# Gates, branches and the last down projection with tokens in the partitions, and both parts of x in one 512-column product of the up projection, in a two-layer decoder trunk

## The chip, the core and the metric

The kernel runs on one core of one Trainium2 chip. The metric is the device time of one execution in microseconds. TensorE is called PE in the views, with its weight loads as PEld; VectorE is DVE, ScalarE ACT, GpSimd POOL, SyncE SP. SP issues the DMAs.

## What is computed

Two layers over 256 tokens of width 1024, all in float32. Each layer has a mixer part and a feed-forward part (FFN):

```python
xn = rms_norm(h, norm_mix[l])
proj = xn @ w_in[l]
(q, k, v, qi, ki, wi, sc_u, sc_b, sc_c, rw_z, gate_pre) = jnp.split(proj, split_points, axis=-1)
...
y_a = dsa_attention(q, k, v, qi, ki, wi)
y_b = short_conv_mixer(sc_u, sc_b, sc_c, sc_conv[l])
y_c = rwkv7_time_mix(rw_z, ...)
branches = jnp.stack([y_a, y_b, y_c], axis=2)
up = jnp.einsum('bsgc,gcd->bsgd', branches, w_branch[l])
gates = jax.nn.sigmoid(gate_pre + b_gate[l]).reshape(bsz, seq, N_BRANCH, D_MODEL)
mixed = jnp.sum(gates * up, axis=2)
h = h + mixed @ w_out[l]
h = h + conv_glu_ffn(rms_norm(h, norm_ffn[l]), ffn_up[l], ffn_conv[l], ffn_down[l])
```

At the end stands `rms_norm(h, norm_final)`. The attention picks 64 keys a query (top-k) with an indexer of its own; the time mixing is a recurrence over the tokens, solved in four chunks of 64; the FFN is 1024 to 2 x 2816, a causal convolution over three tokens, silu(gate) * up, and 2816 back to 1024.

## The kernel before, in words

**Numbers in two parts.** Every float32 operand of a large product is split into a high part in the fp32r format and a low part, the rest. `mm3` makes one product out of three: high weights by high x, low weights by high x, high weights by low x, all into one PSUM bank. A weight block of 128 x 1024 is loaded by SP (`weights`), its high part is a copy on ScalarE or VectorE (CAST 128x1024 in the profile), its low part a subtraction on VectorE (TENSOR_TENSOR 128x1024).

**Layout.** h and everything made from it stand with channels in the partitions and the 256 tokens in the columns. So in `proj` a 128 x 128 block of weights is loaded into PE and 256 columns of x pass it: 8 blocks x 3 = 24 products of 256 columns for 128 output channels. `gate` (8 of these for each of three branches, with the bias and tanh in one ScalarE instruction), `branch` (two outputs from one weight block, 12 products each), the output projection and the FFN's up projection (`proj` or `proj_pair`, 2 a tile) have this form; `down` adds one of 22 tiles into four banks with 24 products of 256 columns. After the last `down` of layer 1 VectorE adds the banks to h, ScalarE scales by the final norm's weights, PE transposes to tokens in partitions, the sum of squares gives the factor, and four DMAs store the result.

**FFN.** Of the 22 tiles the first three (`raw`) are computed from x before its norm is known and scaled afterwards; from the fourth on x is normed first. A tile's down projection follows its up projection by `LAG` = 3 tiles. The convolution reads the bank directly: one ScalarE product, two VectorE SCALAR_TENSOR_TENSOR of 255 and 254 columns.

**Memory.** Tiles of equal size share places, so many for each size: 20 of 4 KB a partition, 5 of 8 KB (x in its two parts, the merged sum), and smaller ones (a gate half is a tile of 1 KB). All 8 PSUM banks are one set.

**Order.** `record` writes down every operation with its dependences; `Program.plan` puts them in an order by the table `STEPS`, whose rows shift priorities, places and the choice between ScalarE and VectorE for operations that either can do; `issue` writes that one order out to all engines. Each engine takes its instructions strictly in this order.

What the change touches, with the lines of the profiled program, follows. Since `issue` writes all instructions (L735), the profile's views name that line throughout, and shapes and tiles tell them apart: `tbank` is a PSUM bank, `t` any shared place.

Of the kernel before, what the change touches and what calls it, by code (L numbers as in the profile page):

```python
# [19 lines left out]
P = 128  # L20
T = 256
# [27 lines left out]
def col_tiles():  # L49
# [8 lines left out]
    gate = lambda b: [(f"g{b}", d, r(O_GATE + DM * b + 128 * d)) for d in range(8)]  # L58
# [10 lines left out]
def branch_after(name, j):  # L69

    if name in ("g0", "g1") and j % 2:
        return [(int(name[1]), j // 2)] + ([(2, dd) for dd in range(4)] if name == "g0" and j == 7 else [])
    return []
# [65 lines left out]
def unit_list():  # L139

    units = []
    for l in range(L):
        for name, j, cols in col_tiles():
            units += [KT * 128]
            units += [4 * 256] * len(branch_after(name, j))
# [8 lines left out]
for _u in UNITS:  # L154
# [4 lines left out]

STEPS = [  # L160
    (1, '', 0, 0, 0, 0, 0), (1, 'ACT', 0, 0, 1.0, 0, 10000000), (2, '', 0, 0, 0, 0, 0), (4, 'places', 0, 0, 0, 0, 0),
    (4, 'places', 0, 0, 0, 0, 0), (4, 'places', 0, 0, 0, 0, 0), (1, 'places', 0, 0, 0, 0, 0),
    (1, 'places', 0, 0, 0, 0, 0), (2, 'engines', 990915, 0, 0.03, 0, 10000000),
    (1, 'order', 896638, 4975, 0.5, 188145, 228145), (1, 'ACT', 217391, 0, 0.3, 595554, 600554),
    (1, 'part', 0, -5023, 0, 1013, 1284), (1, 'part', 0, 4104, 0, 3504, 3576),
    (1, 'order', 923868, 7215, 0.1, 55, 5055), (1, 'part', 0, 1600, 0, 3849, 3933),
    (1, 'order', 288402, 1494, 0.3, 789264, 829264), (1, 'order', 583563, 6230, 0.5, 509266, 549266),
    (1, 'part', 0, -8415, 0, 3683, 3814), (1, 'engines', 587952, 0, 0.03, 692266, 732266),
    (1, 'order', 159137, 7905, 1.0, 706934, 711934), (2, 'kind', 386904, 1641, 0, 0, 10000000),
    (1, 'engines', 488388, 0, 0.1, 615956, 630956), (1, 'engines', 587705, 0, 0.3, 655019, 755019),  # L170
    (1, 'part', 0, -734, 0, 1757, 1772), (1, 'ACT', 181973, 0, 0.3, 693955, 708955),
    (1, 'engines', 364955, 0, 0.01, 0, 10000000), (1, 'engines', 420582, 0, 0.03, 0, 10000000),
    (1, 'engines', 896209, 0, 0.03, 715418, 720418), (1, 'order', 474360, 5710, 0.3, 684381, 699381),
    (1, 'part', 0, 14260, 0, 3707, 3736), (1, 'ACT', 373534, 0, 0.01, 0, 10000000),
    (1, 'order', 542579, 25885, 0.01, 897, 40897), (1, 'engines', 438663, 0, 0.1, 86737, 91737),
    (1, 'ACT', 41472, 0, 1.0, 672478, 712478), (1, 'part', 0, 984, 0, 2447, 2853),
    (1, 'engines', 398618, 0, 0.03, 709685, 809685), (3, 'part', 0, -19735, 0, 1058, 1090),
    (1, 'order', 665662, 2167, 0.1, 144116, 244116), (3, 'engines', 72169, 0, 0.03, 0, 10000000),
    (3, 'order', 130940, 1878, 0.01, 0, 10000000), (1, 'part', 0, 2876, 0, 3891, 4075),
    (1, 'order', 942563, 3016, 0.5, 661837, 701837), (2, 'part', 0, -15687, 0, 63, 91),  # L180
    (1, 'order', 383053, 30450, 1.0, 690456, 695456), (1, 'order', 93525, 1313, 0.01, 0, 10000000),
    (1, 'engines', 831744, 0, 1.0, 108625, 148625), (1, 'part', 0, 2048, 0, 3222, 3261),
    (1, 'engines', 80806, 0, 0.3, 710617, 810617), (1, 'order', 828966, 10709, 0.01, 681522, 721522),
    (1, 'engines', 507078, 0, 0.1, 713036, 728036), (3, 'order', 651912, 3518, 0.03, 0, 10000000),
    (3, 'part', 0, -6283, 0, 564, 651), (2, 'kind', 234875, -743, 0, 0, 10000000),
    (1, 'order', 991842, 2678, 0.03, -7909, 92091), (2, 'order', 347360, 8669, 0.5, 577409, 617409),
    (2, 'part', 0, -822, 0, 3865, 3944), (1, 'engines', 721218, 0, 0.3, 151671, 251671),
    (1, 'engines', 306551, 0, 0.03, 178872, 278872), (1, 'kind', 178191, -1522, 0, -5914, 34086),
    (1, 'engines', 419199, 0, 0.3, 581815, 621815), (1, 'ACT', 794654, 0, 0.3, 634869, 734869),
    (1, 'order', 926129, 13374, 0.03, 64910, 79910), (1, 'ACT', 428750, 0, 1.0, 531114, 571114),  # L190
    (1, 'order', 42072, 10147, 0.01, 557875, 657875), (1, 'engines', 510082, 0, 0.3, 589724, 594724),
    (1, 'part', 0, -950, 0, 3766, 3812), (1, 'order', 147063, 1704, 0.01, 0, 10000000),
    (1, 'part', 0, -19719, 0, 3229, 3240), (1, 'engines', 323590, 0, 0.3, 620245, 635245),
    (1, 'engines', 594072, 0, 0.1, 125838, 140838), (1, 'part', 0, 806, 0, 1233, 1297),
    (1, 'order', 273961, 6202, 0.1, 262736, 362736), (1, 'order', 134846, 3866, 0.01, 0, 10000000),
    (1, 'engines', 95409, 0, 0.3, 979739, 1019739), (1, 'order', 668525, 7708, 0.01, 0, 10000000),
    (1, 'engines', 706667, 0, 0.3, 720429, 725429), (1, 'order', 717637, 7122, 0.03, -19448, 20552),
    (1, 'ACT', 42008, 0, 1.0, 48246, 148246), (1, 'part', 0, -664, 0, 1602, 1651), (4, 'places', 0, 0, 0, 0, 0),
    (1, 'order', 422257, 6239, 0.01, 0, 10000000), (3, 'engines', 105424, 0, 0.1, -13940, 26060),
    (5, 'places', 0, 0, 0, 0, 0), (4, 'places', 0, 0, 0, 0, 0), (2, 'order', 545213, 9838, 0.01, 0, 10000000),  # L200
    (3, 'part', 0, 724, 0, 3539, 3542), (3, 'engines', 473114, 0, 0.03, 0, 10000000),
    (1, 'order', 628496, 37064, 0.03, 644098, 684098), (1, 'part', 0, 3151, 0, 1215, 1230),
    (2, 'order', 290810, 3456, 0.01, 0, 10000000), (3, 'order', 587523, 24879, 0.5, 615132, 655132),
    (1, 'part', 0, -891, 0, 828, 968), (1, 'order', 410355, 36181, 0.3, 603707, 618707),
    (1, 'part', 0, -3528, 0, 1066, 1082), (3, 'order', 706784, 6554, 0.5, 7180, 107180),
    (1, 'ACT', 192201, 0, 1.0, 143721, 183721), (1, 'engines', 50739, 0, 0.03, 597302, 612302),
    (1, 'engines', 703874, 0, 0.03, 0, 10000000), (2, 'engines', 276219, 0, 0.1, 845144, 945144),
    (3, 'order', 765817, 2210, 0.3, 557477, 572477), (1, 'engines', 223121, 0, 0.03, 519497, 619497),
    (1, 'order', 897640, 8500, 0.5, 570780, 610780), (1, 'order', 427450, 6044, 1.0, 705750, 745750),
    (1, 'part', 0, -3754, 0, 3054, 3165), (1, 'engines', 704649, 0, 0.3, 696412, 701412),  # L210
    (1, 'part', 0, 699, 0, 3487, 3531), (1, 'order', 329467, 13522, 0.3, 542936, 582936),
    (1, 'ACT', 810161, 0, 0.3, 473272, 513272), (1, 'order', 143890, 1733, 0.03, 0, 10000000),
    (1, 'ACT', 411363, 0, 0.3, 167522, 267522), (1, 'engines', 606894, 0, 1.0, 575128, 580128),
    (1, 'ACT', 707518, 0, 1.0, 573592, 578592), (1, 'kind', 747229, 10931, 0, 0, 10000000),
    (1, 'order', 779245, 5614, 0.1, 482972, 582972), (1, 'engines', 524910, 0, 0.3, 583218, 598218),
    (1, 'order', 990499, 32354, 0.03, 565786, 665786), (1, 'order', 211927, 3710, 0.5, 178298, 193298),
    (1, 'part', 0, 5170, 0, 553, 561), (1, 'order', 823641, 3167, 0.01, 0, 10000000),
    (1, 'order', 173100, 7368, 0.3, 666551, 706551), (1, 'kind', 268635, 3923, 0, -3950, 36050),
# [1451 lines left out]
```

## Time and profile before

| | before |
|---|---|
| device time, median of 3 runs | 987.15 us (987.07 to 987.45) |
| the profiled execution's own time | 987.48 us |
| its span, first to last instruction | 985.7 us |
| granted PE clock, mean | 0.986 |
| instructions | 21374 |
| DMA, share of 16 engines | 46.8% |

How to read it: a busy time is a share of the span in which an engine had at least one instruction under way. PE's products are pipelined, so a row's mean duration (284 ns for the commonest product) is the latency of one, and the distance between two starts is shorter. "Idle before" is the time an engine rested ahead of the rows of a group, with what ended it. The chain of waits follows the last instruction back to what released it.

### The profile page before, as it was taken

The page shows a single profiled execution, that of the slowest core. Times are in us where ns is not written, and L with a number is a line of the kernel's source. Part 1 is how long each engine was busy: PE and PEld are TensorE (multiplying, and loading weights), DVE is VectorE, ACT ScalarE, POOL GpSimd, SP SyncE. Part 2 cuts the span into 40 slices and gives each one's busy share as a digit, 9 for nine tenths or more (in the row PEclk, how much of TensorE's full clock was granted, in tenths as well). Part 3 has the DMA queues.
Part 4 walks back from the last instruction along what each step waited for, and adds up shares of the span by engine and source line. Part 5 has one row for each costly group of instructions (what it writes and reads, how often), then busy time and mean ns, then how long its engine had stood idle before and what let it go on. Part 6 is the DMA issues. An engine that isn't in the chain of part 4 may idle for free. (4 is left out here: it accounts for less than half of the span.)

```text
span 985.7 us, 21374 instructions
## 1 busy us (share of the span) xinstructions
PE 950.7 (96%) x8692; PEld 925.4 (94%) x8692; DVE 841.9 (85%) x1717; ACT 492.3 (50%) x917; POOL 27.6 (3%) x44
## 2 busy tenths in 40 slices
PE   8999999899999999999998979998999999999996
PEld 7998989899999999999998968997999999999996
DVE  7999859996798986877898997799977999978784
ACT  7954536584255555444766342473843333343443
POOL 1020010000000000000001001000000000000000
PEclk9999999999999999999999989999999999999999
DMA  9443334634653656455533412364255635655541
GB/s 318 155 150 108 100 118 151 213 107 151 211 177 127 195 191 210 164 188 195 206 130 131 169 51 81 124 209 154 99 177 185 212 115 177 211 192 178 187 151 43
DMA packets 45649, 157.93 MB, mean 160 GB/s; under 512 B 5488, under 2 KB 6768, under 8 KB 45552
## 3 DMA queue, kind: packets, MB, share of 16 engines
q1 hardware_dynamic: 45552, 156.58, 46.8%
q8 instruction: 68, 1.11, 0.5%
q14 instruction: 29, 0.24, 0.1%
HBM read 154.99 MB, written 1.05 MB: 158 GB/s over the span
## 5 line engine op out<-in xcount | busy, mean ns | idle before, releaser
L735 PE MATMUL tbank<-t,t 128*128 128x256 f32 (+5 forms) x8440 | 927.0, 276 | 19.5 <-DVE t L735 12.5
L735 PEld LDWEIGHTS tbank<-t,t 128*128 128x128 f32 (+4 forms) x8440 | 901.4, 182 | 39.5 <-issue 14.5
L735 DVE TENSOR_TENSOR t<-t,t 128x1024 fp32r<-128x1024 f32 (+12 forms) x570 | 466.1, 838 | 43.2 <-ACT t L735 34.5
L735 ACT CAST t<-t 128x1024 fp32r<-128x1024 f32 (+3 forms) x335 | 273.8, 837 | 175.7 <-DVE t L735 91.4
L735 DVE SCALAR_TENSOR_TENSOR t<-tbank,tconsts_vec,t 128x255 f32<-128x255 f32 (+1 forms) x168 | 79.4, 480 | 33.7 <-ACT t L735 31.9
L735 ACT ACTIVATE t<-t 128x256 f32<-128x256 f32 (+4 forms) x106 | 44.1, 428 | 73.1 <-DVE t L735 70.5
L735 ACT COPY t<-tbank 128x256 f32<-128x256 f32 (+3 forms) x105 | 45.7, 443 | 59.3 <-PE tbank L735 47.3
L735 DVE SCALAR_TENSOR_TENSOR t<-t,tconsts_vec,t 128x256 f32<-128x256 f32 (+3 forms) x132 | 60.0, 482 | 3.7 <-ACT t L735 3.5
L735 ACT ACTIVATE t<-tbank,tsmall_hv 128x256 f32<-128x256 f32 x64 | 29.4, 473 | 63.4 <-PE tbank L735 63.4
L735 DVE CAST t<-t 128x1024 fp32r<-128x1024 f32 (+2 forms) x86 | 50.6, 595 | 6.4 <-DMA t<-in_w_dram 4.6
L735 ACT ACTIVATE t<-tbank,tconsts_vec 128x256 f32<-128x256 f32 x59 | 27.9, 473 | 49.4 <-PE tbank L735 47.2
L735 ACT ACTIVATE t<-t,tconsts_vec 128x256 fp32r<-128x256 f32 (+1 forms) x56 | 27.0, 502 | 22.5 <-DVE t L735 22.5
L735 PE MATMUL tbank<-tconsts_cst,t 128*128 128x128 f32 (+2 forms) x168 | 27.2, 276 | 6.7 <-DVE t L735 5.3
L735 DVE TENSOR_TENSOR t<-tbank,t 128x256 f32<-128x256 f32 (+2 forms) x52 | 24.4, 478 | 8.4 <-PE tbank L735 5.3
L735 PEld LDWEIGHTS tbank<-tconsts_cst,t 128*128 128x128 f32 (+1 forms) x168 | 20.2, 153 | 8.8 <-issue 3.7
L735 DVE SCALAR_TENSOR_TENSOR t<-t,tbank 128x256 f32<-128x256 f32 x48 | 19.4, 413 | 10.5 <-PE tbank L735 10.4
L735 DVE TENSOR_TENSOR t<-t,tbank 128x256 f32<-128x256 f32 (+1 forms) x48 | 22.8, 484 | 5.9 <-PE tbank L735 5.8
L735 DVE TENSOR_TENSOR t<-t 128x256 f32<-128x256 f32 (+1 forms) x54 | 23.6, 437 | 1.6
L735 POOL TENSOR_SCALAR t<-t 64x4 f32<-64x4 f32 x16 | 10.9, 686 | 446.2 <-DVE t L735 445.4
L735 ACT ACTIVATE t<-t,tatt_mx 128x256 f32<-128x256 f32 (+1 forms) x51 | 21.6, 450 | 0.5 <-DVE tatt_mx L735 0.4
L735 DVE SCALAR_TENSOR_TENSOR t<-t,t 64x252 f32<-64x252 f32 (+3 forms) x42 | 20.4, 506 | 0.3
L735 DVE TENSOR_TENSOR t<-tbank,tconsts_cst 64x256 f32<-64x256 f32 (+1 forms) x48 | 19.3, 419 | 0.7
(85 smaller groups left out, 237.5 us busy)
## 6 DMA issues: line engine op xcount, KB each, us to landing
t<-in_w_dram SPq DMA_DIRECT2D x288, 512.0 KB, 3.6
t<-in_x_dram SPq DMA_DIRECT2D x4, 256.0 KB, 4.0
t<-in_w_dram SPq DMA_DIRECT2D x8, 128.0 KB, 3.6
t<-in_lora_dram SPq DMA_DIRECT2D x4, 256.0 KB, 6.8
out_dram<-t SPq DMA_DIRECT2D x4, 256.0 KB, 2.8
t<-t SPq DMA_DIRECT2D x4, 128.0 KB, 2.4
tconsts_cst<-in_cst_dram SPq DMA_DIRECT2D x1, 339.0 KB, 4.9
t<-in_heads_dram SPq DMA_DIRECT2D x1, 256.0 KB, 7.5
```

The costliest lines, as they stand in the source:

```text
L735: getattr(real[op.engine], name)(*map(arg, args), **{k: arg(v) for k, v in kw.items()})
```

## The change

- **By tokens.** `by_token` loads 128 tokens of x into PE as the fixed operand and lets 512 columns of weights pass: high x by high weights, high x by low weights, low x by high weights. One output is 128 tokens x 512 channels, a full bank. The gates (2 halves a branch, 2 token tiles), the branches and the last layer's down projection (`down_by_token`) take this form. The gates' bias now is a row that a DMA spreads over all partitions; VectorE adds it, ScalarE takes tanh of 1024 columns.
- The gated sum so has tokens in the partitions; PE transposes it back, 16 blocks of 128 x 128 a layer, before the output projection. That projection begins its first three outputs with the first half of the sum.
- **Both parts of x at once.** In the FFN from the fourth tile on, `wide` lets high and low x pass the high weights in one product of 512 columns, into two halves of a bank, and high x pass the low weights in one of 256 columns. The halves are added: a copy (ScalarE or VectorE) and an addition on VectorE; the convolution then reads SBUF.
- **The end.** In layer 1, 16 fp32 products by the identity put h into the down projection's banks; each token tile's banks are squared with a running sum on ScalarE, and VectorE multiplies them by the factor and the norm's row, two DMAs each.
- **Places.** The tiles of 8 KB are gone or halved; nearly all are of 4 KB and share one set. h alone keeps 8 KB.
- **Order.** `STEPS`, `plan` and the cost functions are gone; `FOUND` holds a finished order, the places and the ScalarE or VectorE choice as packed text, and `recall` reads it. `ADDED` is empty, so its branch in `weights` is never taken.

The order on PE at one tile of the second FFN, before: the last rows of a down projection (`tbank_5`, `tbank_1`) and the first of an up product (x is `t2048_4` high and `t2048_1` low, the weights `t1024_18` high and `t1024_1` low):

```order
L735 MATMUL tbank_5_10692<-t1024_4_11705,t1024_6_11845 128x256 x2
L735 MATMUL tbank_5_10692<-t1024_4_11705,t1024_16_11859 128x256
L735 MATMUL tbank_1_10699<-t1024_4_11705,t1024_6_11845 128x256 x2
L735 MATMUL tbank_1_10699<-t1024_4_11705,t1024_16_11859 128x256
L735 MATMUL tbank_4_11999<-t2048_4_10481,t1024_18_11782 128x256
L735 MATMUL tbank_4_11999<-t2048_1_10536,t1024_18_11782 128x256
L735 MATMUL tbank_4_11999<-t2048_4_10481,t1024_1_11797 128x256
```

The same place now: the last rows of an up product into `tbank_2` (`t1024_22` holds both parts of x), then the down projection by tokens:

```order
L487 MATMUL tbank_2_10579<-t1024_22_9351,t1024_7_10469 128x512
L487 MATMUL tbank_2_10579<-t1024_22_9351,t1024_25_10481 128x256
L487 MATMUL tbank_7_9524<-t1024_18_10548,t1024_2_10438 128x512
L487 MATMUL tbank_7_9524<-t1024_27_10559,t1024_2_10438 128x512
L487 MATMUL tbank_7_9524<-t1024_18_10548,t1024_2_10438 128x512
L487 MATMUL tbank_6_9531<-t1024_18_10548,t1024_2_10438 128x512
```

Three products of 256 columns became one of 512 and one of 256 in the up projection, and six became three of 512 in the down projection.

The order on VectorE in layer 1's mixers at the solve of the recurrence (`t1024_19` is its matrix, the STREAM_TRANSPOSE its last transposition), before:

```order
L735 TENSOR_TENSOR t1024_12_7724<-t1024_13_7485,t1024_7_7517 128x1024
L735 TENSOR_TENSOR t256_4_7567<-tbank_1_7679,t256_4_7567 128x256
L735 SCALAR_TENSOR_TENSOR t256_14_7765<-t256_4_7567,tconsts_vec_0_104,t256_14_7765 128x255
L735 SCALAR_TENSOR_TENSOR t256_14_7765<-t256_4_7567,tconsts_vec_0_104,t256_14_7765 128x254
L735 TENSOR_TENSOR t1024_19_7708<-t1024_19_7708,tbank_3_7767 128x16x16
L735 TENSOR_TENSOR t1024_19_7708<-t1024_19_7708,tbank_6_7787 128x16x16
L735 STREAM_TRANSPOSE t1024_9_7817<-t1024_19_7708 128x512
L735 COPY t1024_13_7862<-tbank_0_7826 32x512
```

The same place now (`t1024_26` is the matrix; MAX and MATCH_REPLACE on `tatt_isc0` and `t256_1` are the attention's top-k):

```order
L487 MATCH_REPLACE t256_1_7610<-tatt_m81_0_7809,t256_1_7610 128x256
L487 TENSOR_TENSOR t1024_26_7794<-t1024_26_7794,tbank_1_7873 128x16x16
L487 MAX tatt_m80_0_7915<-tatt_isc0_0_7745 128x8
L487 MAX tatt_m81_0_7809<-t256_1_7610 128x8
L487 TENSOR_TENSOR t1024_26_7794<-t1024_26_7794,tbank_3_7894 128x16x16
L487 MATCH_REPLACE tatt_isc0_0_7745<-tatt_m80_0_7915,tatt_isc0_0_7745 128x128
L487 STREAM_TRANSPOSE t1024_4_7924<-t1024_26_7794 128x512
L487 MAX tatt_m80_0_7915<-tatt_isc0_0_7745 128x8
```

The top-k, which came after the recurrence, now alternates with its solve.

The diff, cut to its core:

```diff
-    gate = lambda b: [(f"g{b}", d, r(O_GATE + DM * b + 128 * d)) for d in range(8)]
+    gate = lambda b: [(f"g{b}", q, list(range(O_GATE + DM * b + 512 * q, O_GATE + DM * b + 512 * q + 512))) for q in range(2)]
...
-STEPS = [
-    (1, '', 0, 0, 0, 0, 0), (1, 'ACT', 0, 0, 1.0, 0, 10000000), (2, '', 0, 0, 0, 0, 0), (4, 'places', 0, 0, 0, 0, 0),
...
+FOUND = (
...
+class Moving:
+    def __init__(self, hi, lo, tiles=()):
+        self.hi, self.lo, self.tiles = hi, lo, tiles
+    def both(self, k):
+        return self.tiles[k // 2][:, k % 2].rearrange("p a t -> p (a t)")
...
-    x8 = pool("x8", 4)
+    x8 = pool("x8", 8)
...
-    gtp = pool("gt", 10)
-    mgp = pool("mg", 1)
+    gtp = pool("gt", 3)
+    rowp = pool("row", 1)
+    mgp = pool("mg", 2)
...
+    def xpair():
+        ts = [x8.tile([P, 2, 2, T], F32R, name="x8") for _ in range(KT // 2)]
+        return Moving(lambda k: ts[k // 2][:, k % 2, 0], lambda k: ts[k // 2][:, k % 2, 1], ts)
...
+    def by_token(x, n):
+        os_ = [pm.tile([P, 512], F32, name="pm") for _ in range(2)]
+        for k in range(n):
+            if k % 2 == 0:
+                wh, wl = weights()
+            s = slice(512 * (k % 2), 512 * (k % 2) + 512)
+            for o, ts in zip(os_, (slice(0, 128), slice(128, 256))):
+                with prog.group("stream"):
+                    PE.matmul(o, x.hi(k)[:, ts], wh[:, s], start=k == 0, stop=False)
+                    PE.matmul(o, x.hi(k)[:, ts], wl[:, s], start=False, stop=False)
+                    PE.matmul(o, x.lo(k)[:, ts], wh[:, s], start=False, stop=k == n - 1)
+        return os_
+    def wide(x):
+        wh, wl = weights()
+        o = pm.tile([P, 2, T], F32, name="pm")
+        for k in range(KT):
+            s = slice(128 * k, 128 * k + 128)
+            with prog.group("stream"):
+                PE.matmul(o.rearrange("p a t -> p (a t)"), wh[:, s], x.both(k), start=k == 0, stop=k == KT - 1, skip_group_check=True)
+                PE.matmul(o[:, 0], wl[:, s], x.hi(k), start=False, stop=k == KT - 1, skip_group_check=True)
+        return o
...
-        def gate(b, d):
-            g = gtp.tile([P, T], F32, name="gt")
-            o = proj(xh, xl)
-            A.activation(g, o, AF.Tanh, bias=hv[:, 8 + 8 * b + d:9 + 8 * b + d], scale=0.5)
+        def gate(b, q):
+            bias = row("bg", 512, (l * 3 + b) * DM + 512 * q)
+            g = gtp.tile([P, 2, 512], F32, name="gt")
+            for tt, o in enumerate(by_token(xn, KT)):
+                V.tensor_tensor(g[:, tt], o, bias, OP.add)
+            A.activation(g, g, AF.Tanh, scale=0.5)
             return g
...
+        def branch(b, q, g):
+            for tt, o in enumerate(by_token(Moving(*(lambda k, t=t: t[:, k] for t in br[b])), 4)):
+                m = mg[tt][:, 512 * q:512 * q + 512]
+                if b == 1:
+                    V.scalar_tensor_tensor(m, g[:, tt], 1.0, o, op0=OP.add, op1=OP.mult)
                 else:
+                    V.scalar_tensor_tensor(g[:, tt], g[:, tt], 1.0, o, op0=OP.add, op1=OP.mult)
+                    V.tensor_tensor(m, m, g[:, tt], OP.add)
+            if b == 2:
+                for d in range(4 * q, 4 * q + 4, 2):
+                    p = pm.tile([P, 2, T], F32, name="pm")
+                    for i in range(2):
+                        for tt in range(2):
+                            PE.transpose(p[:, i, 128 * tt:128 * tt + 128], mg[tt][:, 128 * (d + i):128 * (d + i) + 128], ident)
+                    t = merged.tiles[d // 2]
+                    A.activation(t[:, :, 0], p, AF.Copy, scale=0.5)
+                    V.scalar_tensor_tensor(t[:, :, 1], p, 0.5, t[:, :, 0].bitcast(F32), op0=OP.mult, op1=OP.subtract)
...
+        def down_by_token(item, wd, tts=range(2)):
+            f, ah, al = item
+            wh, wl = wd
+            for tt in tts:
+                ts = slice(128 * tt, 128 * tt + 128)
+                for c in range(2):
+                    o, s = dn[2 * tt + c], slice(512 * c, 512 * c + 512)
+                    with prog.group("stream"):
+                        PE.matmul(o, ah[:, ts], wh[:, s], start=f == 0, stop=False)
+                        PE.matmul(o, ah[:, ts], wl[:, s], start=False, stop=False)
+                        PE.matmul(o, al[:, ts], wh[:, s], start=False, stop=f == FT - 1)
...
-                ps = [proj(xh, xl) for _ in range(2)]
+                ps = [wide(x) for _ in range(2)]
...
+                else:
+                    A.copy(src, ps[e][:, 1])
+                    V.tensor_tensor(src, ps[e][:, 0], src, OP.add)
                 conv(y2[:, e], src, "ffn_conv", FT * e + f, 2 * FT)
...
+        if l == L - 1:
+            for k in range(KT):
+                for tt in range(2):
+                    o = dn[2 * tt + k // 4][:, 128 * (k % 4):128 * (k % 4) + 128]
+                    PE.matmul(o, h[:, k, 128 * tt:128 * tt + 128], ident, start=False, stop=False, skip_group_check=True)
+            wds = [weights() for _ in pend]
+            for tt in range(2):
+                for it, wd in zip(pend, wds):
+                    down_by_token(it, wd, [tt])
+            break
...
-    prog.issue(ctx, tc, prog.plan(STEPS))
+    prog.issue(ctx, tc, prog.recall(FOUND))
```

More of the change, by code (lines that the diff above doesn't have):

```diff
@@ L289 @@
-ENGINES = ("PE", "DVE", "ACT", "POOL", "SP")
-LAT = {("PE", "ACT"): 210, ("PE", "DVE"): 210, ("ACT", "DVE"): 145, ("DVE", "ACT"): 150, ("ACT", "PE"): 275,
-       ("DVE", "PE"): 275, ("DVE", "DVE"): 130, ("ACT", "ACT"): 130, ("POOL", "POOL"): 130, ("PE", "PE"): 0}
-def latency(a, b, raw):
-    if a == b and not raw:
-        return 0
-    return 980 if a == "SP" else LAT.get((a, b), 215)
+NMIX = sum((len(t[2]) + 127) // 128 + 2 * len(branch_after(*t[:2])) for t in col_tiles()) + 8
+ADDED = set()
@@ L301, in other_way @@
+ENGINES = ("PE", "DVE", "ACT", "POOL", "SP", "ADD")
 def other_way(engine, name, args, kw):
@@ L659, in waits @@
-    def waits(self):
-        out = []
-        for o in self.ops:
-            for a, raw in o.preds.items():
-                lat = latency(self.ops[a].engine, o.engine, raw)
-                out.append((a, o.n, lat + (DMA_START if o.engine == "SP" else 0)))
-            for a in o.openers:
-                out.append((a.n, o.n, -a.dur))
-        for rows in self.places.values():
-            for row in rows:
-                for old, new in zip(row, row[1:]):
-                    b = new.users[0]
-                    for o in old.users:
-                        out.append((o.n, b.n, latency(o.engine, b.engine, False) + (DMA_START if b.engine == "SP" else 0)))
-        return out
@@ new lines, in record, with some @@
+        for b in (1, 0):
+            for q in range(2):
+                branch(b, q, gate(b, q))
+        merged = xpair()
+        for q in range(2):
+            branch(2, q, g2[q])
+        u = None
+        ahead = [(weights(), pm.tile([P, T], F32, name="pm")) for _ in range(3)]
+        def some(d, ks):
+            (wh, wl), o = ahead[d]
+            for k in ks:
+                s = slice(128 * k, 128 * k + 128)
+                mm3(o, wh[:, s], wl[:, s], merged.hi(k), merged.lo(k), k == 0, k == KT - 1)
@@ L1506, in record @@
+        for d in range(3):
+            some(d, range(4))
+        for d in range(KT):
+            if d < 3:
+                some(d, range(4, KT))
+                o = ahead[d][1]
+            else:
+                o = proj(merged)
             V.tensor_tensor(h[:, d], h[:, d], o, OP.add)
-            if uh is None:
-                uh, ul = xtile("uh"), xtile("ul")
-            raw_split(vc("norm_ffn", d), d, uh, ul)
+            if u is None:
+                u = xpair()
+            raw_split(vc("norm_ffn", d), d, u)
@@ L1638, in layout @@
                     wb = wb[perm]
-                put_w(rows(wb[:, 256 * dd:256 * dd + 256]))
+                for p in range(2):
+                    put_w(rows(wb[:, 512 * q:512 * q + 512])[:, 2 * p:2 * p + 2])
         for d in range(KT):
```

615 lines of the change are left out of this document (192 added, 423 removed).

## The prediction

> **What bounds the kernel now.** I read the page first, then the busy time by stage, the chain of waits and PE's own waits. The page:
>
> ```profile
> span 985.7 us, 21374 instructions
> PE 950.7 (96%) x8692; PEld 925.4 (94%) x8692; DVE 841.9 (85%) x1717; ACT 492.3 (50%) x917; POOL 27.6 (3%) x44
> ```
>
> The busy time by stage, cut where the chain and the additions to h show the ends: layer 0's mixers, its FFN, layer 1's mixers in two parts, its FFN, the end (columns: us, then busy time and instructions of PE, weight loads, DVE, ACT, POOL, then the granted clock). The last row is a stretch inside the second FFN:
>
> ```profile
> 0.00:300.00 300.00, 289.72 (x2755) 276.25 (x2756) 261.13 (x582) 174.71 (x355) 16.61 (x31) 0.98 0.48 166
> 300.00:484.00 184.00, 184.00 (x1558) 184.00 (x1557) 149.00 (x249) 92.30 (x146) 0.00 (x0) 1.00 0.53 181
> 490.00:684.70 194.70, 177.76 (x1829) 166.99 (x1829) 173.58 (x408) 94.38 (x176) 10.99 (x13) 0.96 0.39 131
> 684.70:787.50 102.80, 102.77 (x892) 102.16 (x893) 88.24 (x163) 49.74 (x102) 0.00 (x0) 1.00 0.50 169
> 787.50:970.20 182.70, 182.70 (x1551) 182.70 (x1550) 156.13 (x275) 68.62 (x113) 0.00 (x0) 1.00 0.50 165
> 970.20:985.70 15.50, 7.77 (x67) 7.30 (x65) 8.19 (x29) 6.51 (x14) 0.00 (x0) 0.89 0.20 68
> 800.00:850.00 50.00, 50.00 (x425) 50.00 (x424) 49.86 (x96) 16.77 (x30) 0.00 (x0) 1.00 0.51 171
> ```
>
> From 684.7 us to 970.2 PE never rests, and both FFNs are PE's alone. Where it rests is the mixers: 10.3 us in layer 0 (300 - 289.7), 16.9 us in the first part of layer 1 (194.7 - 177.8). VectorE is next in line: 81% of the first FFN, 85% of the second. The chain of waits and PE's waits say the same:
>
> ```profile
> 684.73 285.51 PE tbank L735 x2438
> PE tbank L735 <- DVE t L735: 17.8, 17, 3.5
> ```
>
> So a microsecond taken from PE's stream after 684.7 us or in an FFN shortens the run, as long as VectorE keeps up.
>
> **The price of a product.** Shapes of the whole run (count | busy us, mean ns | idle before it, and what ended it):
>
> ```profile
> L735 PE MATMUL tbank<-t,t 128*128 128x256 f32 x7000 | 865.5, 284 | 8.5 <-DVE t L735 5.0 <-ACT t L735 3.1
> L735 PE MATMUL tbank<-t,tconsts_cst 128*128 128x512 f32 x8 | 3.8, 592 | 0.0
> ```
>
> A row's mean is the latency of one; what counts is the distance between starts. In the second FFN it is 182.70 / 1551 = 117.8 ns for 256 columns. The change turns pairs of these into one of 512 columns. No such product in this number format is in the trace; two views bound it: the timeline of PE in a spell of half clock (with the shapes in it), and the timeline of the one 512-column shape there is, in fp32 (4 products in the order, 8 records on the page):
>
> ```profile
> 81.32 1.91 PE L735 MATMUL tbank<-t,t 128*128 128x256 f32 x8
> 81.60:84.40 2.80, 2.80 (x15) 0.50 0.88 300
> L735 PE MATMUL tbank<-t,t 128*128 128x256 f32 x15 | 3.4, 414 | 0.0
> 140.65 1.88 PE L735 MATMUL tbank<-t,tconsts_cst 128*128 128x512 f32 x4
> ```
>
> At half clock eight starts are (1.91 - 0.414) / 7 = 213.7 ns apart, so 256 columns alone need 213.7 / 2 = 106.9 ns at full clock, and the 117.8 hold 11 ns that are not columns. At half clock these 11 ns vanish behind the longer stream, although a weight load stands before every product. The fp32 records of 512 columns start (1.88 - 0.592) / 3 = 429 ns apart; if each passes its columns twice, 512 columns take 214.7. Taken: 215 ns, between the two. The other end is 235.6, twice 117.8; in the middle lies 224.8, where each instruction keeps its 11 ns.
>
> The Trainium skill speaks against the change here: "TensorE: Matmul & The Clock Gate", section "Back-to-back issue gap", gives columns / 2.4 plus 2.5 ns, thus 109.2 and 215.8 ns, and a pair would save 2.5 ns, 4.3 us in all. The trace does not agree: 117.8 against 109.2.
>
> **The change part by part.** The built program holds 1736 products of 512 columns in place of 3472 of 256: gates 288 and branches 144 a layer, the last down projection 264, the up projection 304 a layer. *Stream*: 1736 x (235.6 - 215) = -35.8 us.
>
> *Added on PE.* The gated sum now has tokens in its partitions and is transposed back: 16 a layer. The h of the last layer goes into the down projection's banks by 16 fp32 products of 128 columns. The 16 transposes of the old end go, but they lay behind VectorE's chain there. Rows of the old end (timeline):
>
> ```profile
> 971.85 0.41 DVE L735 TENSOR_TENSOR t<-t,tbank 128x256 f32<-128x256 f32 x1
> 972.18 0.42 DVE L735 TENSOR_TENSOR t<-t,t 128x256 f32<-128x256 f32 x1
> 974.96 3.01 PE L735 MATMUL tbank<-tconsts_cst,t 128*128 128x128 f32 x24
> 975.18 0.42 DVE L735 TENSOR_TENSOR t<-t,tbank 128x256 f32<-128x256 f32 x1
> 977.08 0.16 DVE L735 TENSOR_SCALAR ttiny_nx<-tbank 128x2 f32<-128x2 f32 x1
> 978.90 2.42 ACT L735 ACTIVATE t<-tbank,ttiny_ny 128x512 f32<-128x512 f32 x4 [3.12 <-DVE ttiny_ny L735]
> ```
>
> A transpose is at most 3.01 / 24 = 0.13 us: 32 make 4.0. An fp32 product of 128 columns is an estimate from the fp32 row: two records of 429 / 4 ns, 0.21 us, 16 make 3.4. Both on the path: **+7.4 us**.
>
> *The end.* From the last addition to h (975.18) to 985.7 it is 10.5 us. Now each half of the tokens is squared out of its banks on ScalarE, goes through the same small steps (977.08 to 978.90, 1.8 us, and one addition of 0.2), two multiplications, and the same way out (981.3 to 985.7, 4.4). With the rows of 512 columns below (0.61 ScalarE, 0.68 VectorE): 0.6 + 2.0 + 1.4 + 4.4 = 8.4 for the second half, the first lying ahead of it. **-2.1 us**.
>
> *VectorE and ScalarE.* The rows that carry this:
>
> ```profile
> L735 DVE TENSOR_TENSOR t<-tbank,t 128x256 f32<-128x256 f32 x40 | 16.3, 418 | 5.4 <-PE tbank L735 5.3
> L735 DVE COPY t<-tbank 128x256 f32<-128x256 f32 x9 | 3.8, 421 | 3.1 <-PE tbank L735 3.0
> L735 DVE CAST t<-t 128x1024 fp32r<-128x1024 f32 x66 | 45.2, 688 | 6.0 <-DMA t<-in_w_dram 4.6 <-PE tbank L735 1.3
> L735 DVE TENSOR_TENSOR t<-t,tbank 128x512 f32<-128x512 f32 x12 | 8.0, 684 | 1.4 <-PE tbank L735 1.4
> L735 DVE SCALAR_TENSOR_TENSOR t<-t,tbank 128x256 f32<-128x256 f32 x48 | 19.4, 413 | 10.5 <-PE tbank L735 10.4
> L735 DVE TENSOR_TENSOR t<-t 128x256 f32<-128x256 f32 x53 | 22.4, 422 | 1.4
> L735 ACT ACTIVATE t<-tbank 128x512 f32<-128x512 f32 x16 | 8.8, 608 | 2.7 <-PE tbank L735 2.7
> L735 DVE SCALAR_TENSOR_TENSOR t<-tbank,tconsts_vec,t 128x255 f32<-128x255 f32 x92 | 43.9, 480 | 32.2 <-ACT t L735 31.9
> ```
>
> An up product of the new form leaves two halves in a bank, which are added: 38 copies and 38 additions a layer. By the built order VectorE gets in the first FFN 38 additions, 12 of the copies and 14 more weight casts: 38 x 0.418 + 12 x 0.421 + 14 x 0.688 = 30.6 us, to 179.6 busy by row durations, against PE's new 184 - 304 x 0.0206 = 177.7. In the second it is 38 additions, 20 copies and 7 casts fewer: 19.5 us, to 175.6, against 182.7 - 568 x 0.0206 + 3.4 = 174.4. That looks full, but the rows overlap: of the old end's rows one of 0.41 us is followed by the next start after 0.33. With 0.08 us less for each of some 60 added instructions it is about 174 and 171, and the 249 and 275 old ones have more of that overlap to give where they stand closer. The 50 us with VectorE at 49.86 and PE at 50.00 show that a full VectorE need not starve PE. I take +1.5 us an FFN for stalls, **+3**; the ends are 0 and the rival below.
>
> In the mixers the gates' bias, once ScalarE's, is 12 VectorE additions of 512 columns a layer; the branches take 12 + 8 of 512 for 24 + 16 of 256: 12 x 0.684 + 20 x 0.684 - 24 x 0.413 - 16 x 0.422 = +5.2 us a layer, on an engine with some 20 to 40 us of room there. It ends nowhere on the path while gates and branches are filler.
>
> *Order.* Before, the solve of the recurrence in layer 1 and the top-k of the attention stand one after the other on VectorE, and PE runs out of filler in both (16.9 us). Now they alternate, with gate and branch products of 512 columns beside them. After the last recurrence product, the order before has 2803 stream products left (x 117.8 = 330 us), now 640 + 718 (x 117.8 and x 215 = 230 us): the chain may end 100 us nearer the end and PE still has work. Against it, there is less filler by 432 x 0.0206 = 8.9 us a layer. Between 0 and all of the 27.2 us of rest can go, or some be added; I take 7 of it, a quarter: **-7**. The common set of 4 KB places and the bias rows' 12 loads cost nothing here: the DMA share is about half in every stage, and loads run ahead.
>
> *Sum*: -35.8 + 7.4 - 2.1 + 3 - 7 = -34.5. The profiled run took 987.5 us around its span of 985.7, 0.3 above the median of 987.15; I leave that, and 987.5 - 34.5 gives **953 us**.
>
> **The rivals.**
> 1. *All rest goes*: the mixers run without a gap, 20 us more than taken: 933. For it: both chains now overlap. Against: the start and the two norms have no filler.
> 2. *The excess stays with each instruction*: 224.8 ns, 1736 x 9.8 = 17 us back: 970. Against: the half-clock row hides it.
> 3. *The cost goes with the columns*: 235.6 ns, nothing saved: 953 + 35.8 = 989, within 0.2% of before. Against: both bounds. The skill's rule named above comes out near it, 4.3 us lower, 985.
> 4. *VectorE takes the FFN in part*: a third of its old idle time there stays, as it waits for ScalarE in its fixed order: old idle time is 35.0 + 26.6 us; 20 us not absorbed: 973.
> 5. *VectorE becomes the bound* (slower): every up product now waits twice for ScalarE, for the copy and for the convolution's first term, and the 32.2 us of such waits do not shrink. Then an FFN is VectorE's added-up time and its waits: 179.6 + 35.0 = 214.6 against 177.7, and 175.6 + 26.6 = 202.2 against 174.4, +64.7: 1018. It decides from 34.5 us on, half of these waits. Against: most of that idle time is slack that exists because PE is slower, and the four banks that the down projection leaves and its lag of three tiles absorb a late result.
>
> **How the numbers follow.** A difference under 0.2%, 2 us, could not be told from none. Forecast 0.58, of itself good for 943 to 963 (rest and stalls). Rival 1: 0.10; 2: 0.10; 3: 0.04; 4: 0.12; 5: 0.06. The range goes from 936, most of rival 1, to 974, which takes in 2 and 4 and leaves out 3 and 5. Faster: all but 3 and 5, and a little of 3: 0.91. Same: 0.03. Slower: 0.06.
>
> **What would show it.** Right: the 512-column row 213 to 218 ns from start to start; FFNs of about 179 and 176 us with PE full and VectorE over 93%; PE's rest before the last recurrence product under 22 us; about 8.4 us from the last product to the end. Wrong: 512 columns at 224 or more; "PE <- DVE" or "PE <- ACT" waits inside an FFN of over 5 us; a chain that ends in VectorE rows within an FFN.

## The result, and the profile after

The changed kernel takes 962.69 us (median of 4 runs, 961.7 to 964.26) beside 987.3 us for the kernel before on the same chip: ratio 0.975, interval 0.9733 to 0.9767, or 24.7 us less. The forecast said 953 us, with 936 to 974 as its range.

The page of the kernel after, its first rows and the row of the clock:

```profile
span 960.3 us, 17959 instructions
PE 938.1 (98%) x6996; PEld 833.8 (87%) x6996; DVE 883.5 (92%) x1836; ACT 481.3 (50%) x871; POOL 27.5 (3%) x44
PEclk8999999999999999999999999999999999999998
```

The span fell by 25.4 us. PE is busy 12.6 us less and rests 22.2 us (960.3 - 938.1) in place of 35.0, so rest gave 12.8, the other half. The forecast had given rest 7 of its 34.5 us and had looked for the remainder in the stream.

The stages, with the same columns as before: layer 0's mixers, its FFN, layer 1's mixers in two parts, its FFN to 950 us (2.3 us before PE's last product ends), the end.

```profile
0.00:297.30 297.30, 287.69 (x2338) 251.99 (x2339) 273.64 (x607) 157.01 (x290) 16.43 (x31) 0.98 0.52 173
297.30:482.00 184.70, 184.70 (x1274) 171.30 (x1273) 174.38 (x329) 84.22 (x154) 0.00 (x0) 1.00 0.58 190
490.00:652.00 162.00, 157.91 (x1278) 145.81 (x1277) 149.90 (x329) 90.16 (x155) 7.75 (x9) 0.99 0.49 153
652.00:763.70 111.70, 111.27 (x993) 93.45 (x992) 102.25 (x207) 56.83 (x111) 3.33 (x4) 1.00 0.51 161
763.70:950.00 186.30, 186.30 (x1045) 161.76 (x1044) 171.27 (x339) 83.73 (x144) 0.00 (x0) 1.00 0.50 161
950.00:960.30 10.30, 2.25 (x10) 1.50 (x8) 4.11 (x14) 1.38 (x4) 0.00 (x0) 0.74 0.27 102
```

Two things are to be seen. The first FFN takes 184.7 us, not less than the 184.0 of before, although 304 of its pairs of narrow products (256 columns) are now single wide ones (512 columns); PE is busy in all of it. The two stretches do not hold quite the same work: 1274 + 304 = 1578 narrow products' worth against 1558, and 20 narrow ones are 2.4 us, so that like for like some 1.7 us went where the forecast had 304 x 0.0206 = 6.3. And layer 1's mixers end at 763.7 where they ended at 787.5: PE rests 4.1 + 0.4 us there in place of 16.9.

The widths explain the first. PE's timeline in a stretch that holds only 512-column products, and the two shapes over the whole run:

```profile
532.24 13.48 PE L487 MATMUL tbank<-t,t 128*128 128x512 f32 x57
```

```profile
L487 PE MATMUL tbank<-t,t 128*128 128x256 f32 x3528 | 536.7, 285 | 10.3 <-DVE t L487 10.2
L487 PE MATMUL tbank<-t,t 128*128 128x512 f32 x1736 | 489.4, 397 | 0.2 <-DVE t L487 0.2
```

The last of 57 products takes its latency of 0.397 us, the 56 before it (13.48 - 0.397) / 56 = 233.6 ns each from start to start (the median over the run is 232). The forecast took 215; two narrow ones take 2 x 118. So a wide product saves 4 ns over its pair of narrow ones, and not 20.6.

PE's waits and the chain, against 17.8 us and 285.51 us of before:

```profile
PE tbank L487 <- DVE t L487: 11.3, 13, 3.6
```

```profile
689.64 261.93 PE tbank L487 x1612
```

The chain's long last PE piece is shorter by 23.6 us, begins 5 us later and so ends 18.7 us earlier. As the order is another, it begins at another place of the work, and its length alone does not say where the time went.

The end, from the timeline:

```profile
947.82 4.44 PE L487 MATMUL tbank<-t,t 128*128 128x512 f32 x18
950.49 6.29 SPq L487 DMA_DIRECT2D out_dram<-t  x4
951.59 0.60 ACT L487 ACTIVATE t<-tbank 128x512 f32<-128x512 f32 x1 [3.92 <-PE tbank L487]
955.02 1.41 DVE L487 SCALAR_TENSOR_TENSOR t<-tbank,ttiny_ny,t 128x512 f32<-128x512 f32 x2
```

The last product ends at 952.26, the run at 960.3: 8.0 us (forecast 8.4).

**Where 25.4 us went.** The trace has the start of each product. Of each distance from one start to the next I take off the time in which no product ran (rest), and half of what lay in half-clock time (lost to the clock); the remainder is the product's own price. (Half is a little too much, as at half clock 256 columns were 213.7 ns apart and not 2 x 118; this shifts under 0.5 us between the rows of a difference.) Sums in us; the third column is the first experiment below.

| | before | after | after, with halves |
|---|---|---|---|
| products of 256 and 512 columns | 846.4 | 835.9 | 844.1 |
| other products | 93.3 | 95.3 | 95.3 |
| rest from the first product to the last | 26.1 | 12.6 | 12.1 |
| lost to half clock | 10.7 | 6.5 | 10.6 |
| before the first start, after the last | 9.1 | 9.9 | 10.0 |
| span | 985.7 | 960.3 | 972.2 |

### The profile page after: what moved, and what is told of

The parts are those of the page before. It is cut to its first block, busy times and chain, and to the rows that moved or that the text cites. A ratio compares the mean times of both kernels' runs of the same rounds, so it can differ in the third digit from the quotient of the medians.

```text
span 960.3 us, 17959 instructions
## 1 busy us (share of the span) xinstructions
PE 938.1 (98%) x6996; PEld 833.8 (87%) x6996; DVE 883.5 (92%) x1836; ACT 481.3 (50%) x871; POOL 27.5 (3%) x44
## 4 chain that ended last, share of the span: by engine, by line
PE 80%; DVE 14%; ACT 2%; issue 2%; DMA 1%; SPq 0%; DVEq 0%; ACTq 0%
PE tbank L487 80%; DVE t L487 13%; ACT t L487 2%; DMA t<-in_w_dram 1%; SPq L487 0%; DMA t<-in_x_dram 0%; DVE tatt_mx L487 0%; DVE ttiny_na L487 0%; DVE tatt_isc L487 0%; DVE ttiny_ny L487 0%; DVE tatt_m L487 0%; DVEq L1493 0%; DVE ttiny_nx L487 0%; DVEq L487 0%; ACTq L1493 0%
## 5 line engine op out<-in xcount | busy, mean ns | idle before, releaser
L487 PE MATMUL tbank<-t,t 128*128 128x256 f32 (+7 forms) x6704 | 913.3, 304 | 11.0 <-DVE t L487 10.6
L487 PEld LDWEIGHTS tbank<-t,t 128*128 128x128 f32 (+5 forms) x6704 | 803.9, 179 | 105.8 <-DVE t L487 12.4
L487 DVE TENSOR_TENSOR t<-t,t 128x1024 fp32r<-128x1024 f32 (+11 forms) x548 | 456.9, 862 | 9.2 <-ACT t L487 7.9
L487 ACT COPY t<-tbank 128x256 f32<-128x256 f32 (+3 forms) x139 | 57.6, 422 | 171.3 <-PE tbank L487 153.9
L487 DVE SCALAR_TENSOR_TENSOR t<-t,tconsts_vec,t 128x254 f32<-128x254 f32 (+3 forms) x284 | 131.1, 480 | 2.0 <-ACT t L487 1.2
L487 ACT ACTIVATE t<-t,tconsts_vec 128x256 f32<-128x256 f32 (+1 forms) x104 | 51.1, 506 | 66.9 <-DVE t L487 66.5
L487 DVE TENSOR_TENSOR t<-tbank,t 128x256 f32<-128x256 f32 (+2 forms) x152 | 72.1, 482 | 10.2 <-PE tbank L487 5.5
L487 DVE COPY t<-tbank 128x256 f32<-128x256 f32 (+3 forms) x63 | 28.6, 455 | 21.2 <-PE tbank L487 17.1
L487 PEld LDWEIGHTS tbank<-tconsts_cst,t 128*128 128x128 f32 (+1 forms) x208 | 25.4, 153 | 6.8 <-DVE t L487 2.1
L487 ACT ACTIVATE t<-t,tatt_mx 128x128 f32<-128x128 f32 (+1 forms) x55 | 22.9, 443 | 2.5 <-DVE tatt_mx L487 2.3
L487 DVE SCALAR_TENSOR_TENSOR t<-t,tbank 128x512 f32<-128x512 f32 x24 | 16.3, 684 | 5.4 <-PE tbank L487 5.4
L487 DVE TENSOR_TENSOR t<-t 128x256 f32<-128x256 f32 x47 | 19.6, 420 | 1.2 <-DMA t<-in_x_dram 0.6
```

Source lines behind the costliest of these rows:

```text
L487: getattr(real[op.engine], name)(*map(arg, args), **{k: arg(v) for k, v in kw.items()})
```

## The experiments

All times below stand as ratios to the kernel before on the same chip, since the chips differ by a microsecond or so; 0.1% is 1 us.

**1. The width alone, undone.** In each group of the stream, shortened (the product of `wide` is divided in the same way):

```
-  PE.matmul(o, x.hi(k)[:, ts], wh[:, s], start=k == 0, stop=False)
+  for i in range(2):
+      c = slice(256 * i, 256 * i + 256)
+      PE.matmul(o[:, c], x.hi(k)[:, ts], wh[:, s][:, c], start=k == 0 and i == 0, stop=False)
```

> The kernel after, with each of its 1736 products of 512 columns as two of 256 in the same place of the same order; nothing else is altered. It is the width alone, undone. The forecast's theory (512 columns take 215 ns, a pair of 256 takes 235.6): 1736 x 20.6 ns = 35.8 us slower than the kernel after, about 998 us, slower than the kernel before. The rival read off the profile of after (512 columns take 232 ns, the cost goes with the columns): 1736 x 4 ns = 6.9 us slower, about 969.5 us, so that some 18 us of the change's gain are still there without any wide product. Middle case (224.8 ns each): 19 us, 981.5 us.

Measured: 973.56 us, ratio 0.986 (0.9841 to 0.9879), 1.1% or 10.9 us above the kernel after. Its page and its stream:

```profile
span 972.2 us, 21398 instructions
PE 950.4 (98%) x8732; PEld 927.2 (95%) x8732; DVE 884.0 (91%) x1836; ACT 481.0 (49%) x871; POOL 27.5 (3%) x44
```

```profile
L487 PE MATMUL tbank<-t,t 128*128 128x256 f32 x7000 | 865.1, 284 | 10.5 <-DVE t L487 10.4
```

This is the same 7000 products and the same 950 us of busy PE as before the change, and yet 13.5 us less: rest 21.8 (972.2 - 950.4) where before had 35.0. So over half of the gain is there with no wide product at all: it is what the new order, the places and the other forms bring together, which this run does not separate. In the table, the width is worth 8.2 us of stream, 4.7 ns a pair; the other 4.1 us of this run's distance is more time at half clock, and for it the time lies 4 us above the 969.5 expected from 4 ns a pair. The forecast's 35.8 us is refuted, and so is the middle case's 19.

**2. The price of one product, alone.** A kernel of nothing but products; the names are r (fp32r), b (bf16), v (fp32r beside VectorE and ScalarE), d (beside loads), e (fp32r again).

> Only PE's products, nothing of the reference: back-to-back products with a new weight tile each, on an otherwise idle core: 224 in fp32r with 256 columns, 96 with 512, 96 with 128; then 96 in bf16 with 256 and 96 with 512; then 96 in fp32r with 512 while VectorE and ScalarE each cast 16 tiles of 1024 columns; then 96 with 512 while 12 loads of 512 KB run; then 96 with 256. Read: distance from start to start at full clock. If the excess of 11 and 18 ns over the columns at 2.4 per ns is contention with the other engines' or the transfers' traffic, fp32r takes 109 and 214 to 216 ns on the idle core and more only in the loaded stretches. If it belongs to fp32r (its data or its weights, by the column), it takes 117 and 231 ns on the idle core too, and bf16 109 and 214 to 216. If it is the clock itself under a long full load, bf16 shows it as well.

```profile
L36 PE MATMUL r<-xr,wr 128*128 128x512 f32 x96 | 21.9, 390 | 0.0
L36 PE MATMUL v<-xr,wr 128*128 128x512 f32 x96 | 22.2, 392 | 0.0
L36 PE MATMUL d<-xr,wr 128*128 128x512 f32 x96 | 21.9, 390 | 0.0
L36 PE MATMUL b<-xb,wb 128*128 128x512 bf16 x96 | 20.9, 379 | 0.0
L36 PE MATMUL e<-xr,wr 128*128 128x256 f32 x96 | 11.7, 283 | 0.0
L36 PE MATMUL r<-xr,wr 128*128 128x128 f32 x96 | 10.8, 275 | 0.0
L36 PE MATMUL b<-xb,wb 128*128 128x256 bf16 x96 | 10.7, 273 | 0.0
```

(Busy less one latency) / 95 gives the distance: fp32r (21.9 - 0.39) / 95 = 226.4 ns for 512 columns, 120.2 for 256, 110.8 for 128; bf16 216.0 and 109.8. The row v gives 229.6, but its first start stands only 29 ns behind the last one of b; from its eleventh distance on it is 227 like the others.

From 256 to 512 columns both formats grow by 106.2 ns, so 120.2 - 106.2 = 14.0 ns of an fp32r product and 3.6 of a bf16 one are not columns. The excess is there on an idle core, comes with fp32r, and is the same for 256 and 512. It did not vanish behind the longer stream, which is what the forecast had read out of the half-clock row. Whether the product or the load of its weights brings it was not separated, since both changed format together and every product in these runs has its load:

```profile
L36 PEld LDWEIGHTS d<-xr,wr 128*128 128x128 f32 x96 | 18.0, 188 | 3.7
L36 PEld LDWEIGHTS <-wb 128*128 128x128 bf16 x192 | 18.7, 98 | 12.2
```

A load shows as 188 ns in fp32r and as 98 in bf16. With 128 columns the distance hardly falls below that of 256 (110.8 and 120.2), so there it is not the columns that set it.

The formula of the Trainium skill that the prediction weighed ("TensorE: Matmul & The Clock Gate", section "Back-to-back issue gap", where it is given for the isolated single product; estimates by it are 109.2 and 215.8 ns) agrees with the bf16 rows, 109.8 and 216.0, and not with the fp32r ones. Its saving for the whole kernel, 4.3 us, was nearer to the 8.2 us of experiment 1 than the forecast's 35.8 was, but by prices that neither fp32r nor this kernel has.

**3. What the kernel's 232 has over 227.** Two more kernels of products alone.

> Only PE's products in fp32r, nothing of the reference, to see what the kernel's 232 ns have over the 227 of the idle core: 200 of 256 columns; 120 of 512 with two moving tiles and two banks in turn; 120 with a moving tile of zeros; 60 with two moving tiles while VectorE subtracts 1024-column tiles, ScalarE casts such tiles and six loads of 512 KB run; 100 of 256 columns, most beside the same load; 100 of 512 columns with one tile, idle again. If the traffic of the other engines is the cause, only the loaded stretch shows 232; if it is the change of the moving tile or of the bank, the second shows it already; if it is the data's toggling (less clock), zeros take less than 227.

```profile
L41 PE MATMUL zero<-xz,wr 128*128 128x512 f32 x120 | 27.4, 389 | 0.0
L41 PE MATMUL idle<-xr,wr 128*128 128x512 f32 x100 | 22.9, 389 | 0.0
```

The stretch of 60 products with VectorE, ScalarE and loads beside it, from the windows:

```profile
86.50:99.90 13.40, 13.40 (x60) 11.09 (x60) 12.22 (x11) 12.08 (x12) 0.00 (x0) 1.00 0.35 119
```

Zeros (27.4 - 0.389) / 119 = 227.0; idle 227.4; loaded 13.4 / 59 = 227; two moving tiles and two banks in turn, 120 products that start from 32.12 to 59.35 us, 27.23 / 120 = 226.9. Neither traffic nor data nor the change of tile and bank, as tried here, is the cause.

> Only fp32r products, nothing of the reference, in the patterns of the kernel: 200 of 256 columns as a start; 99 of 512 in threes, of which two use one weight tile and two moving tiles alternate; 160 that alternate between 512 and 256 columns; 99 of 256 in threes; 60 of 512 alone; 60 of 512 and 60 of 256 while VectorE and ScalarE read another bank of PSUM without a pause. In the kernel a pair of 512 and 256 takes 232 + 117 = 349 ns, 512 after 512 takes 232 and 256 after 256 takes 118; alone it was 227 and 120. If the pattern makes the difference, the threes or the alternating ones show the kernel's numbers; if reads of PSUM do, the last two show them; if neither does, it stays open.

```profile
L40 PE MATMUL mixed<-xr,wr 128*128 128x512 f32 x80 | 28.3, 398 | 0.0
L40 PE MATMUL idle<-xr,wr 128*128 128x512 f32 x60 | 13.8, 389 | 0.0
L40 PE MATMUL bank<-xr,wr 128*128 128x512 f32 x60 | 13.8, 389 | 0.0
```

Alternating 512 and 256, as the up projection does, takes (28.3 - 0.398) / 79 = 353 ns a pair, more than 227 + 120 = 347 and than the kernel's 349: there a pattern alone can bring the difference. For 512 after 512 the threes settled at 227 after their first five (233, 236, 228, 233, 231), and reads of PSUM changed nothing. Why the kernel stays at 232 in its pure stretches is open. It is only 5 ns of 232, but it decides what the width is worth: bare, a wide product saves 2 x 120.2 - 226.4 = 14.0 ns over two narrow ones, 24 us for 1736; in the kernel, where the wide one takes 5 ns more and the narrow ones 2 ns less, 8.2 us.

**4. The two chains of layer 1, left out of both kernels.** `times` is how often an operation is issued; the order is made with it and then the instruction left out. In short, for the top-k; the solve's 45 stand between the same two lines:

```
+  prog.times = 1 - l
   V.max(m8, acc)
   V.match_replace(acc, m8, acc, TAKEN)
+  prog.times = 1
```

> The kernel before, in its own order, without 77 VectorE instructions of layer 1: the 16 pairs of maximum and replacement of the top-k (some 12 us busy) and the 45 of the solve's 15 steps (some 13 us). It leaves that part of the computation out. If the order's gain comes from PE's rest and half clock beside these two chains, this kernel gets most of that gain without the new order: PE rests 12.1 us in the two stretches that hold them (7.2 around the solve, 4.9 around the top-k) and has 10.2 us of half clock there; 10 to 16 us faster than before, about 971 to 977 us. If layer 1's gain has nothing to do with the chains (other filler, other places for buffers), under 4 us faster, above 983 us.

> The kernel after without the same 77 instructions of layer 1, left out in its own order. If the new order hides both chains behind products, leaving them out brings only what rest is left beside them, 3.6 us, and at most 1.7 us of half clock: 0 to 5 us faster than the kernel after, 957 to 962 us. If the chains still set the time, as much as in the kernel before: 10 us or more, under 952 us.

Measured: the kernel before gets 8.4 us faster without them (ratio 0.9915, 0.9898 to 0.9931), the kernel after 3.6 (0.9714, 0.9688 to 0.974, against 0.975). The expectation for the first was 10 to 16: a miss in size. Windows of the kernel before around the start of layer 1, the solve and the top-k, then of before without the chains:

```profile
489.00:560.00 71.00, 67.52 (x575) 65.37 (x573) 66.06 (x131) 43.65 (x77) 4.47 (x8) 0.98 0.45 155
560.00:625.00 65.00, 57.78 (x828) 51.17 (x831) 52.88 (x139) 22.80 (x47) 6.52 (x5) 0.95 0.21 67
665.00:690.00 25.00, 20.08 (x161) 19.14 (x161) 24.93 (x81) 8.10 (x18) 0.00 (x0) 0.93 0.46 152
```

```profile
489.00:560.00 71.00, 67.54 (x566) 65.52 (x566) 65.85 (x130) 43.77 (x78) 4.47 (x8) 0.95 0.43 152
560.00:625.00 65.00, 61.14 (x876) 54.37 (x875) 46.80 (x91) 25.18 (x51) 6.53 (x5) 1.00 0.26 85
665.00:690.00 25.00, 22.95 (x202) 22.46 (x201) 20.76 (x40) 14.82 (x46) 0.00 (x0) 1.00 0.39 139
```

PE's rest falls from 7.2 to 3.9 us at the solve and from 4.9 to 2.0 at the top-k, and the clock in both goes back to 1.00. In the stretch ahead of them it falls from 0.98 to 0.95 of 71 us, behind the same rest of 3.5 us, which takes some 2 us of the gain back. The rest that stays is that of steps around the 77 instructions, and the 3.5 us at the layer's start are not touched.

**5. The chains set one after the other again, in the kernel after.** The order is written out anew, once as it is and once with a rule; instructions, engines and places stay. The rule in short (the kernel holds only the order that came of it):

```
+  edges = [(first_recurrence_step, top_k[0]), (first_recurrence_step, top_k[1])]   # layer 1
```

> The kernel after, its order written out anew by a list scheduler that takes the old order as priorities: the same instructions, engines and places, and nearly the same order. It is the measure for the next run: within 4 us of the kernel after, 959 to 967 us.

> The same as the run before with one added rule: the two top-k loops of layer 1 (and what depends on them) come on VectorE only after the solve and the first step of the recurrence; products and everything else may move up. The chains of layer 1 stand one after the other again, nearer to the kernel before; widths, instructions and places are unchanged. If alternating the chains is what took PE's rest out of layer 1, rest comes back: 8 to 17 us slower than the run before, 970 to 980 us, with new waits of PE for VectorE between 640 and 710 us. If the gain of the order lies elsewhere (start of the layer, other filler), under 4 us slower.

Measured: the order written anew 968.03 us, ratio 0.9797 (0.9782 to 0.9812), 1 us outside what was expected; with the rule 983.41, ratio 0.9945 (0.9924 to 0.9966): 14.6 us slower. Windows of 590 to 640 and 640 to 720 us, first without the rule, then with it:

```profile
590.00:640.00 50.00, 47.58 (x402) 44.38 (x402) 49.58 (x134) 28.32 (x55) 2.01 (x1) 1.00 0.49 144
640.00:720.00 80.00, 80.00 (x857) 62.39 (x856) 73.86 (x179) 47.06 (x96) 3.16 (x4) 1.00 0.45 140
```

```profile
590.00:640.00 50.00, 47.57 (x407) 44.40 (x406) 49.58 (x133) 28.30 (x55) 2.02 (x1) 1.00 0.48 147
640.00:720.00 80.00, 70.99 (x784) 57.29 (x782) 64.59 (x158) 39.27 (x84) 3.86 (x4) 0.91 0.41 124
```

Up to 640 us the two are alike. Then PE rests 9.0 us where it rested not at all, and the clock falls to 0.91 of 80 us, 7 us more: together 16 us, where the spans differ by 15.3 (981.6 and 966.3). VectorE stands on one chain while PE has run out of filler, the products that wait for neither chain, and the rest is paid a second time in the half clock behind it.

So the order's gain hangs on where the top-k stands. By the traces its maxima and replacements run from 668.7 to 685.4 us before, where the solve's last transposition starts at 592.0, and from 644.0 to 670.7 now, where it starts at 652.4: the two alternate over its last 8 us, and the rest of the top-k runs beside what follows. The size is less clear. Leaving the 77 instructions out took 8.4 us from the kernel before and 3.6 from the kernel after, so they account for 4.8 of some 14 us; the rule also held back what depends on the top-k.

**6. Two terms of the sum.** VectorE's margin in the FFN (`prog.times = 2` around the subtraction of the split), and the h products (`prog.times = 0` around them).

> The kernel after, in which 22 subtractions of 128x256 a layer in the FFN (the low part of the activation) are issued twice, with the same result: 22 x 0.42 us = 9.2 us more VectorE work in each FFN, where VectorE is busy 174 of 185 us. If a VectorE that is busy 94% still leaves PE its pace (the forecast's reason), 0 to 4 us slower than the kernel after. If its waits for ScalarE are part of its path (the two VectorE rivals of the forecast), the whole addition shows: 15 to 18 us slower, about 979 us.

Measured: ratio 0.9764 (0.9749 to 0.978), 1.4 us above the kernel after, which the intervals do not tell from none. Its first FFN:

```profile
297.80:484.00 186.20, 185.55 (x1275) 171.48 (x1274) 182.41 (x352) 85.10 (x154) 0.00 (x0) 1.00 0.60 188
```

VectorE is busy 182.4 of 186.2 us and PE rests 0.65 us. In the second FFN (764 to 951 us) VectorE is busy 180.2 of 187.0 us and PE does not rest. A nearly full VectorE hardly slows these FFNs.

> The kernel after without the 16 fp32 products of 128 columns that put the last layer's h into the banks of the down projection; h is left out of the result. They stand in PE's stream just before the end, where PE never rests. The forecast's term (0.21 us each, on the path): 3.4 us faster than the kernel after, about 959 us, ratio 0.9715. If each costs one record of 109 ns: 1.7 us, 0.973. If they fall into a rest that exists anyway: nothing.

Measured: ratio 0.971 (0.9692 to 0.9728), 0.4% or 4 us less than the kernel after. The row of this shape, which has 188 records in the kernel after:

```profile
L489 PE MATMUL tbank<-tconsts_cst,t 128*128 128x128 f32 x156 | 25.2, 276 | 1.3 <-ACT t L489 0.7 <-DVE t L489 0.6
```

32 records fewer, two for each product, at 109 ns (the median distance behind a record of this shape): 3.5 us. The time alone, 2 to 6 us by its interval, would not tell 3.4 from 1.7; the records do. The term of 3.4 us held.

## Why the prediction was right, and where it was not

The time was inside the range and just inside the forecast's own 943 to 963, but by luck: it came out of two errors that point opposite ways. The sum, term by term, forecast against the table:

- **Stream, -35.8: wrong.** Measured -10.5, of which the width undone shows 8.2. The step that failed is "At half clock these 11 ns vanish behind the longer stream", from which 215 ns was taken. On the idle core the excess of 14 ns stays with each fp32r product at full clock; in the kernel 232 leaves 20 beside 2 x 106.2. The row at half clock says what two things take when the columns are slow; it does not say that the longer product at full clock hides the same. The second bound, the fp32 row, is of another format, and experiment 2 shows that the excess goes by format. Rivals 2 (224.8 ns) and 3 (235.6) enclose the measured 232; the sign that the prediction named for "wrong", 224 or more, was there.
- **Order, -7: wrong in size, right in kind.** Rest fell by 13.5 and the loss to half clock by 4.2, together 17.7. With halves, in the same order, rest fell by 14.0 and the loss to half clock by 0.1, so only the rest is sure. The reason was as given, the two chains alternating with filler beside them; experiment 5 takes it away and loses 14.6. "A quarter of the 27.2 us of rest" was a choice between 0 and all, and half went; the clock's share was not in the sum at all, though the profile of before has six half-clock windows in the mixers.
- **FFN stalls, +3: not there.** No wait of PE stands in either FFN, and 9 us more VectorE work in each costs 1.4 us. VectorE was busy 174.4 and 171.3 us, as estimated (174 and 171), 94% and 92% of the two stretches (over 93% was said). Rivals 4 and 5, VectorE in part or wholly the bound, are refuted; the reason that the lag and the four banks absorb late results held.
- **Added products and end, +7.4 - 2.1: about right.** The h products are 3.5, 32 transposes at 109 ns 3.5, the end 8.0 in place of 10.5. In the table "other products" grow by 2.0 alone, in part because 16 transposes of the old end went too, and start and end by 0.8.
- **FFNs of 179 and 176 us: wrong**, 184.7 for the first and 186.3 for the second up to 950 us, by the price of the product.

Together: stream 25.3 us short of forecast, order 10.7 beyond it, stalls 3 and the small terms 2.5 less cost: 25.3 - 10.7 - 3 - 2.5 = 9.1, from -34.5 to -25.4. With the measured price and the forecast's own other terms the sum would have been 987.5 - 34.5 + 25.3 = 978, outside the range; mostly the order's size brought the result to 963.

What stays open: the 5 ns between 227 and 232; whether the excess of fp32r lies in the product or in the load of its weights; how much of the 4.2 us of clock is this order's doing, since time at half clock differs between runs of one kernel (below; the mean clock was 0.986 in 30 executions of the kernel before and 0.989 in 21 of the five kernels with the order of after, some 3 us); and the rest at layer 1's start (3.5 us before, 0.45 after from 484 to 590), which went with the order but was not tried by itself.

## What to carry to other kernels

A price that the trace does not show should be measured by a chain of bare products before a sum hangs on 1736 of it: one such run would have moved this forecast's largest term from 36 us to 16 (235.6 - 226.4 = 9.2 ns each). It would not have given the 8 that the kernel showed, so a bare price shows what is possible and not what the kernel pays. When a change alters both the work and its order, run the old work in the new order; here that one run showed that over half of the gain came without the wide products. And count rest on the bounding engine twice where a rest is followed by half clock.

## What the runs showed of the hardware

- fp32r products with a new weight tile each took 110.8, 120.2 and 226.4 ns for 128, 256 and 512 columns on the idle core, bf16 109.8 and 216.0 for 256 and 512. Other engines' load, transfers, zeros in the data and reads of PSUM did not change the fp32r numbers (227 for 512 columns); alternating 512 and 256 columns took 353 ns a pair where 347 would be the sum.
- Half clock came in stretches of 3.41 us or two or three times that, apart from the last of each trace, which begins behind PE's last product. In the nine traces of whole kernels each of them had 1.5 us of PE's rest or more in the 8 us ahead of it. The same place drew different lengths: with a rest of 3.6 us near 610 us the kernel after had 3.41 us and the kernel with halves 6.83. In the same order the loss ranged from 5.0 us (the subtraction twice) to 10.7 (without the h products); the five runs without the h products had mean clocks of 0.985 to 0.992 and times of 962.6 to 958.4 us. The spread between runs of one kernel goes in part with the clock.
- VectorE at 98% busy (182.4 of 186.2 us) beside a PE that rests 0.65 us: here a nearly full engine off the path cost 1.4 us of the whole run, less than the intervals can show.
